# Partition sums of an adaLN modulation: four narrow matmuls and a transposition per 512 columns, or 32x32 block transpositions and one matmul per section

## The chip, the cores and the metric

The kernel runs on one core of a Trainium2 chip. The metric is device time of one execution in microseconds (us). Three runs of the kernel before took 1637.54, 1637.94 and 1638.12 us; their median is 1637.94 us.

## The reference

Two transformer blocks on one sequence of 512 tokens and 1024 features, all in float32. Each block has its own modulation: six vectors of 1024 values (shift, scale and gate for the mixer and for the feed-forward part), from a conditioning vector `c`:

```python
mod = (jax.nn.silu(c) @ w_ada[i] + b_ada[i])[:, None, :]
shift_m, scale_m, gate_m, shift_f, scale_f, gate_f = jnp.split(mod, N_MOD, axis=-1)
h = rmsnorm(x, norm_mix_w[i]) * (1.0 + scale_m) + shift_m
x = x + gate_m * hybrid_mixer(h, ...)
h = rmsnorm(x, norm_mlp_w[i]) * (1.0 + scale_f) + shift_f
x = x + gate_f * (jnp.square(jax.nn.relu(h @ w_up[i])) @ w_down[i])
```

`w_ada` is 1024 x 6144, so a modulation is a vector times a matrix of 25 MB. The second block has the same form, with an mLSTM and sliding-window attention as its mixer and a gated convolutional feed-forward part. The mixer of the first block is a state-space scan (heads of 64 features, chunks of 128 tokens) with a pooling branch.

## The kernel before

Large products are made exact in float32 by splitting each operand into a high and a low part of type float32r: `hilo` (lines 238 to 244) lets ScalarE copy the raw weights into `whi` (L242) and VectorE subtract (L243, `wlo`). `gemm_a` (L273) and `gemm_full` (L351) then issue three matmuls of 512 columns for every 128x128 weight tile. Weights arrive by SyncE's DMA queue in tiles `wraw` of four buffers (`RAW`).

The modulation is a side stream that is fed between the weights. `split_w` calls `pump` after every tile of weights, and every `pump_rate[0]`-th call lets `ada_next` emit one step: a DMA of 512 KB of `w_ada` (four k-tiles of 256 columns, L150) and four VectorE instructions that multiply the rows by the values of `silu(c)` and add them up in an accumulator `adacc` (128 partitions x 256 columns; L154 for the first, L156 for the rest). Two steps make one accumulator of two 128-column pieces. What is left is a sum over the 128 partitions. `ada_sum` does it for four pieces at a time:

```python
for j in range(4):
    PE.matmul(ps[j * 32:(j + 1) * 32, 0:P], lhsT=ones[:, 0:32], rhs=accs[j // 2][:, j % 2 * P:(j % 2 + 1) * P],
              start=True, stop=True)
row = small("colraw", [P, P])
act(out=row, in_=ps[:, 0:P], func=AF.Copy)
```

These are four matmuls with a weight of ones, 32 columns wide, each into its own quarter of the PSUM partitions (L163). Then come a copy on ScalarE (L166), a transposition on TensorE (L169) and an addition of the bias on VectorE (L170) that leaves four columns of `mod`. A section (1024 values) is two such sums. `ada_close` delays sums so that the steps of one lie apart. `ada_until` closes all that is open before a section is used: section 2 of the first block before `GM`, sections 4 and 3 before `g_f`, section 5 before `GF`; sections 0 and 1 of the second block before `gc1`, sections 2, 4 and 3 before `gc2`, section 5 at the end before `G2`. The flag `hold` keeps `gemm_full` from starting new sums, and `ADB - 1` accumulators are the most that may be open, `ADB` being 5.

The shift and scale of the very first normalization are not part of this stream: `first_mod` (L499 to L512) makes them at the start, one pair of pieces for each of eight k-tiles, with two accumulators from the same five buffers and four matmuls (L505).

The tile framework places the instructions of each engine in an order that it plans; every engine runs its own list in order. The front of each norm is of interest below: `front1` (L1024, L1025) adds the gated output of the mixer to `x`, and `h_tile` (L423 to L432) transposes the normalized tokens, scales them and splits them into `hh` (ScalarE) and `hl` (VectorE, L432), which `first_tiles` multiplies by the first weights of the MLP in halves of 256 tokens. Other lines named below: L243 `wlo`, L261 and L357 weight DMAs, L449 the convolution `xs`, L414 the normalized tokens `nx`, L867 the sum of squares over partitions (four full-width float32 matmuls of one column), L1313 a maximum over 512 scores, L1499 the last addition of `post`.

Of the kernel before, what the change touches and what calls it, by code (L numbers as in the profile page):

```python
# [26 lines left out]
def hybrid_kernel(  # L27
# [46 lines left out]
    # ---------------------------------------------------------------- constants  # L74
# [27 lines left out]
    def first_ada(j):  # L102
        """the pieces j of the shift and the scale of the first normalization, four k-tiles at a time."""
        res = []
        for k, tag in ((0, "hi"), (4, "lo")):
            u = wp.tile([P, 4, 2 * P], F32, tag=tag, name="araw")
            for i in range(2):
                dma(out=u[:, :, i * P:(i + 1) * P],
                    in_=w_ada[0, k * P:(k + 4) * P, (8 * i + j) * P:(8 * i + j + 1) * P].rearrange("(k p) n -> p k n", p=P))
            res.append(u)  # L110
        return res
# [29 lines left out]
    # ---------------------------------------------------------------- adaLN modulation  # L141
    mod = [const("mod1", [P, 48]), const("mod2", [P, 48])]
    ada_w, bcol = [w_ada, w_ada_2], [ba_col, None]

    def ada_steps(ci, col):
        """steps that sum the products of the 128-column pieces col and col + 1 of w_ada over their k-tiles."""
        acc = small("adacc", [P, 2 * P], bufs=ADB)
        for k0 in (0, 4):
            raw = RAW([P, 4, 2 * P])
            dma(out=raw, in_=ada_w[ci][0, k0 * P:(k0 + 4) * P, col * P:(col + 2) * P].rearrange("(k p) n -> p k n", p=P))  # L150
            for k in range(4):
                s_ = csil[:, 8 * ci + k0 + k:8 * ci + k0 + k + 1]
                if k0 + k == 0:
                    V.tensor_scalar(out=acc, in0=raw[:, k], scalar1=s_, scalar2=None, op0=ALU.mult)  # L154
                else:
                    V.scalar_tensor_tensor(out=acc, in0=raw[:, k], scalar=s_, in1=acc, op0=ALU.mult, op1=ALU.add)  # L156
            yield acc

    def ada_sum(ci, col, accs):
        """the sums over partitions of four pieces, as columns."""  # L160
        ps = PS("adaps")
        for j in range(4):
            PE.matmul(ps[j * 32:(j + 1) * 32, 0:P], lhsT=ones[:, 0:32], rhs=accs[j // 2][:, j % 2 * P:(j % 2 + 1) * P],  # L163
                      start=True, stop=True)
        row = small("colraw", [P, P])
        act(out=row, in_=ps[:, 0:P], func=AF.Copy)  # L166
        yield
        ps = PS("adaps")
        PE.transpose(ps[:, 0:P], row, ident)  # L169
        V.tensor_tensor(out=mod[ci][:, col:col + 4], in0=ps[:, 0:P:32], in1=bcol[ci][:, col:col + 4], op=ALU.add)  # L170
        yield

    ada_todo = [(0, 8 * sec + i) for sec in (2, 4, 3, 5) for i in range(0, 8, 2)] + [(1, i) for i in range(0, 48, 2)]
    ada_now, ada_open, ada_half = [], [], []
    pump_rate = [0, 0]

    def pump():
        """half a piece of the modulation for every pump_rate[0] tiles of weights."""
        pump_rate[1] += 1
        if pump_rate[0] and pump_rate[1] % pump_rate[0] == 0:  # L180
            ada_next()

    def ada_close(n):
        while ada_half:
            next(ada_half.pop(0))
        while len(ada_open) > max(n, 1):
            (ci, col), a0 = ada_open.pop(0)
            ada_half.append(ada_sum(ci, col, (a0, ada_open.pop(0)[1])))
            next(ada_half[-1])
        while ada_half and n == 0:  # L190
            next(ada_half.pop(0))

    def ada_next(hold=False):
        if ada_now:
            key, gen = ada_now.pop()
            ada_open.append((key, next(gen)))
            return
        if not hold:
            ada_close(3)
        if ada_todo and len(ada_open) < ADB - 1:  # L200
            ci, col = ada_todo.pop(0)
            ada_now.append(((ci, col), ada_steps(ci, col)))
            next(ada_now[0][1])

    def ada_until(ci, sec):
        todo = [(ci, 8 * sec + i) for i in range(0, 8, 2)]
        while any(t in todo for t in ada_todo + [t for t, _ in ada_now]):
            ada_next()
        ada_close(0)

    def cols_to_dram(name, col):
        """[P, n] columns -> n rows in DRAM."""
# [9 lines left out]
    def rows_bcast(name, dr, r0):  # L222
        """four rows of 128 from r0 on, the same in every partition."""
# [4 lines left out]
    def cols_to_rows(name, col):  # L228
        """[P, 8] columns -> two [P, 512] tiles with the vector in every row, by way of DRAM."""
# [8 lines left out]
    # ---------------------------------------------------------------- products  # L238
# [7 lines left out]
    def split_w(parts, kt=8):  # L246
        """weights [kt * 128, 256] (in column parts) -> per k-tile (hi, lo)."""
# [29 lines left out]
    def load_b(wmat, cols, k0):  # L277
        """two k-tiles of the columns [(first, number)] of wmat."""
# [8 lines left out]
    def keep(raw):  # L287
        """weights split into tiles that stay."""
# [10 lines left out]
    def gemm_b(wmat, acts, cols, evac, pairs=((0, 1, 2, 3),), ready=()):  # L299
        """[tokens, columns] products, at most 512 columns, in steps of two k-tiles; with several token groups  # L300
        the weights are held; the first k-tiles of the weights may be there already."""
# [35 lines left out]
    def gemm_full(wmat, acts, evac, tail=4, groups=((0, 1), (2, 3)), before=None, script=None):  # L337
        """[tokens, 1024] products of acts [(row tile, (hi, lo))]; the last `tail` k-tiles go by token
        groups, so that evac(group, pss) of one overlaps the products of the next; before(i) is called
        after k-tile i."""  # L340
# [77 lines left out]
    def h_tile(xh, j, p, ts, gc, bc, on_act=False, bank=PS):  # L418
        """features j of the tokens ts: transposed, scaled, shifted and split into p."""
# [14 lines left out]
    def first_tiles(ws, acts, between=None):  # L434
        """products of the first two 256-column weights, by token halves."""
# [8 lines left out]
    def conv(ps, name, cols, taps, b):  # L444
        """depthwise causal convolution of a [features, tokens] product; cols[k] are [P, 1]."""
# [7 lines left out]
    def silu2(u):  # L453
        """silu(2u), in place."""
# [4 lines left out]
    def log1p_exp_negabs(y, n, name):  # L459
        """log(1 + exp(-|y|)) of [P, n] with the relative accuracy of float32."""  # L460
# [15 lines left out]
    # ================================================================ block 1: mixer  # L476
# [68 lines left out]
    # parameters of the convolution  # L545
# [30 lines left out]
    # time steps: the k-tiles in four column groups of the tensor engine, summed with the transposition  # L576
# [14 lines left out]

    def xbc_items(g):
        """closures that add the convolved tiles of group g to XBC[g]."""
# [19 lines left out]
    # pool branch  # L613
# [30 lines left out]
    # remaining parameters  # L644
# [67 lines left out]
    # time steps  # L712
# [47 lines left out]
    # state-space branch, a group of eight heads at a time  # L760
# [3 lines left out]
    def ssd_decay(g, cc, st):  # L764
        """what chunk cc of group g needs besides the state: scaled inputs, decayed scores, decayed C."""
# [54 lines left out]
    def ssd_out(g, cc, st):  # L820
        """the outputs of chunk cc of group g and the state after it."""
# [32 lines left out]
    def rms_stages(tiles, eps, wcol, name, res):  # L854
        """tiles [features, tokens] -> normed over all their features, scaled by wcol, split, added to res."""
# [43 lines left out]
    def branch_items(g):  # L899
        """the groups g - 1 and g."""  # L900
# [35 lines left out]
    def weave(stages, items):  # L936
        """emits the stages with the items [(cost, step)] spread evenly between them."""
# [760 lines left out]
```

## Time and profile before

| what | value |
|---|---|
| median of three runs | 1637.94 us (1637.54 to 1638.12) |
| profiled execution, first to last instruction (span) | 1635.9 us |
| TensorE (PE), busy | 1605.5 us, 98% |
| TensorE weight loads (PEld), busy | 1293.6 us, 79% |
| VectorE (DVE), busy | 1069.6 us, 65% |
| ScalarE (ACT), busy | 721.2 us, 44% |
| GpSimd (POOL), busy | 28.1 us, 2% |
| chain that ended last | PE 93%, DVE 2%, DMA 2%, ACT 1%, issue 1% |
| mean granted TensorE clock | 0.998 |
| HBM read, written | 202.96 MB, 2.19 MB |

The profile gives the span of the profiled execution and not its own time around it; the median of the runs is 2.04 us above the span. "Busy" of TensorE is modelled from pipelined matmuls, so that consecutive ones overlap in the rows: the step from one start to the next tells what a matmul costs, the duration of one row does not. A float32 matmul is recorded as two rows, a float32r matmul and a transposition as one.

### The profile page before, as it was taken

The numbers are of one execution on the slowest core, as the hardware profiler recorded it, in microseconds if no ns is written. First come the engines' busy times: TensorE is split into PE (matmuls) and PEld (weight loads), VectorE is DVE, ScalarE is ACT, GpSimd is POOL, SyncE is SP. The second block draws the span as 40 slices with busy tenths as digits, with TensorE's granted clock in tenths as the row PEclk, the third lists the DMA queues.
The fourth block names the chain that finished last, engine by engine and source line by source line (L and its number), as shares of the span: only waits on it lengthen the run. The fifth ranks groups of instructions, "written<-read, shape, count | busy, mean of one in ns | idle before, by whom it ended". The sixth has DMA issues, their size and how long they took to land.

```text
span 1635.9 us, 21014 instructions
## 1 busy us (share of the span) xinstructions
PE 1605.5 (98%) x7942; PEld 1293.6 (79%) x7942; DVE 1069.6 (65%) x1944; ACT 721.2 (44%) x1279; POOL 28.1 (2%) x46
## 2 busy tenths in 40 slices
PE   5999999999999999999999999999999999999998
PEld 3778777777877878877877788878888888888886
DVE  6686898889676676875267654584576756245644
ACT  3543665555454333533123333646555544144421
POOL 0000000000000000000000000000001000000000
PEclk9999999999999999999999999999999999999999
DMA  9632544454544444565246571132232333332321
GB/s 284 185 104 66 174 142 142 130 160 132 158 129 142 129 140 144 167 201 185 91 143 194 181 242 27 53 93 62 72 105 71 90 91 103 91 103 82 99 90 52
DMA packets 206762, 206.52 MB, mean 126 GB/s; under 512 B 11397, under 2 KB 184645, under 8 KB 206661
## 3 DMA queue, kind: packets, MB, share of 16 engines
q1 hardware_dynamic: 206661, 205.19, 40.6%
q8 instruction: 62, 1.02, 0.3%
q14 instruction: 39, 0.32, 0.1%
HBM read 202.96 MB, written 2.19 MB: 125 GB/s over the span
## 4 chain that ended last, share of the span: by engine, by line
PE 93%; DVE 2%; DMA 2%; ACT 1%; issue 1%; POOL 0%; SPq 0%; DVEq 0%; POOLq 0%; ACTq 0%
PE ga L273 54%; PE gb L351 21%; PE gb L311 5%; PE go L1480 2%; PE ga L543 2%; DMA wraw<-in_w_ada_dram 1%; PE yps L831 1%; PE ops L1343 1%; PE stps L840 1%; PE nps L423 1%; PE sps L1310 1%; PE yps L836 1%; PE adaps L163 0%; PE xtps L792 0%; PE ptps L1334 0%
## 5 line engine op out<-in xcount | busy, mean ns | idle before, releaser
L243 DVE TENSOR_TENSOR wlo<-wraw,whi 128x1024 fp32r<-128x1024 f32 (+3 forms) x249 | 298.0, 1198 | 256.3 <-ACT whi L242 256.0
L273 PE MATMUL ga<-hh,whi 128*128 128x512 f32 (+1 forms) x1200 | 465.2, 390 | 0.3 <-ACT hh L430 0.3
L273 PE MATMUL ga<-hl,whi 128*128 128x512 f32 (+1 forms) x1200 | 459.2, 384 | 3.0 <-DVE hl L432 2.9
L273 PE MATMUL ga<-hh,wlo 128*128 128x512 f32 (+1 forms) x1200 | 458.0, 382 | 0.0
L242 ACT ACTIVATE whi<-wraw 128x1024 fp32r<-128x1024 f32 (+3 forms) x249 | 257.8, 1036 | 341.2 <-PE ga L273 152.1
L273 PEld LDWEIGHTS ga<-hl,whi 128*128 128x128 f32 x1200 | 226.0, 189 | 52.4 <-DVE hl L432 3.9
L273 PEld LDWEIGHTS ga<-hh,whi 128*128 128x128 f32 x1200 | 224.6, 188 | 53.2 <-issue 6.4
L273 PEld LDWEIGHTS ga<-hh,wlo 128*128 128x128 f32 x1200 | 226.1, 189 | 47.1 <-issue 0.3
L156 DVE SCALAR_TENSOR_TENSOR adacc<-wraw,csil,adacc 128x256 f32<-128x256 f32 x280 | 133.6, 482 | 30.9 <-DMA wraw<-in_w_ada_dram 26.4
L351 PE MATMUL gb<-whi,hidh 128*128 128x512 f32 x240 | 78.2, 396 | 0.0
L351 PE MATMUL gb<-wlo,hidh 128*128 128x512 f32 x240 | 77.8, 395 | 0.0
L351 PE MATMUL gb<-whi,hidl 128*128 128x512 f32 x240 | 77.5, 394 | 0.0
L449 DVE SCALAR_TENSOR_TENSOR xs<-xraw,colB,xs 128x511 f32<-128x511 f32 (+2 forms) x72 | 53.9, 748 | 9.1 <-ACT xs L447 8.3
L351 PE MATMUL gb<-whi,fh 128*128 128x512 f32 x176 | 57.1, 395 | 0.0
L351 PE MATMUL gb<-wlo,fh 128*128 128x512 f32 x176 | 57.1, 394 | 0.0
L351 PE MATMUL gb<-whi,fl 128*128 128x512 f32 x176 | 56.9, 393 | 0.0
L351 PEld LDWEIGHTS gb<-whi,hidh 128*128 128x128 f32 x240 | 45.0, 188 | 10.8 <-issue 0.4
L351 PEld LDWEIGHTS gb<-whi,hidl 128*128 128x128 f32 x240 | 45.1, 188 | 10.7
L351 PEld LDWEIGHTS gb<-wlo,hidh 128*128 128x128 f32 x240 | 45.1, 188 | 10.5
L805 ACT ACTIVATE arel<-AB,acs 128x128 f32<-128x128 f32 x128 | 40.7, 389 | 26.8 <-DMA AB<-acs 18.8
L273 PE MATMUL ga<-yh,whi 128*128 128x512 f32 x128 | 51.3, 401 | 0.0
L273 PE MATMUL ga<-yl,whi 128*128 128x512 f32 x128 | 50.5, 394 | 0.0
(417 smaller groups left out, 2398.3 us busy)
## 6 DMA issues: line engine op xcount, KB each, us to landing
wraw<-in_w_ada_dram SPq DMA_DIRECT2D x80, 512.0 KB
wraw<-in_w_in_dram SPq DMA_DIRECT2D x72, 512.0 KB
wraw<-in_w_down_dram SPq DMA_DIRECT2D x54, 512.0 KB
wraw<-in_w_up_dram SPq DMA_DIRECT2D x88, 256.0 KB
wraw<-in_w_up_dram SPq DMA_DIRECT2D x32, 512.0 KB
araw<-in_w_ada_dram SPq DMA_DIRECT2D x32, 256.0 KB
AB<-acs SPq DMA_DIRECT2D x32, 256.0 KB
wraw<-in_w_branch_ssd_dram SPq DMA_DIRECT2D x16, 512.0 KB
```

Source lines behind the costliest of these rows:

```text
L156: V.scalar_tensor_tensor(out=acc, in0=raw[:, k], scalar=s_, in1=acc, op0=ALU.mult, op1=ALU.add)
L242: act(out=hi, in_=raw, func=AF.Copy)
L243: V.tensor_tensor(out=lo, in0=raw, in1=f(hi), op=ALU.subtract)
L273: PE.matmul(ps[:, n0:n1], lhsT=a[:, m * P:(m + 1) * P], rhs=b[:, n0:n1], start=i == 0, stop=i == 3 * n - 1)
L311: PE.matmul(pss[t][:, 0:ncols], lhsT=a[:, t * P:(t + 1) * P], rhs=b, start=k == 0 and j == 0, stop=k == n - 1 and j == 2)
L351: PE.matmul(pss[t][q], lhsT=a, rhs=w[b][q], start=i == 0 and j == 0, stop=i == n - 1 and j == 2)
L423: PE.transpose(ps[:, i * P:(i + 1) * P], xh[t][j // 4][:, (j % 4) * P:(j % 4 + 1) * P], ident)
L449: V.scalar_tensor_tensor(out=o[:, d:], in0=ps[:, 0:S - d], scalar=cols[taps - 1 - d], in1=o[:, d:], op0=ALU.mult, op1=ALU.add)
L543: PE.matmul(fps[i], lhsT=a[:, i * P:(i + 1) * P], rhs=b, start=j == 0 and q == 0, stop=j == 7 and q == 2)
L805: act(out=t[:, i * P:(i + 1) * P], in_=AB[q][:, i * P:(i + 1) * P], func=AF.Relu, scale=-1.0, bias=acs[:, hh:hh + 1])
L831: PE.matmul(ps[r * 64:(r + 1) * 64, j * P:(j + 1) * P], lhsT=xdt[:, hh * 64:(hh + 1) * 64], rhs=M[hh // 4][:, (hh % 4) * P:(hh % 4 + 1) * ...
L1480: PE.matmul(opss[t][q], lhsT=x_, rhs=w[q][b_], start=half == 0 and k == 0 and j == 0, stop=half == 1 and k == 3 and j == 2)
```

## The change

The partition sum moves from TensorE to VectorE. A unit of the stream is now four pieces in one accumulator of 128 x 512 from the general pool `U` (64 buffers). After its fourth step a VectorE block transposition turns each 32x32 block of the accumulator (`adtr`), and a VectorE reduction adds 32 values each, which leaves 16 columns of `adR`: the sums of each group of 32 partitions. Only when a section is wanted does `ada_until` issue one matmul of 32 columns with a full 128x128 weight `quarters` (made of identity blocks), which adds the four groups for all 1024 values of the section, and three short VectorE instructions: a product with the mask `quarter`, a reduction, the bias. `ada_close`, `ada_sum` and the limit on open accumulators go away, and `hold` no longer has an effect. `first_mod` keeps its form, but `ADB`, the number of its accumulator buffers, falls from 5 to 3. Two small constants are made at the start.

```diff
     def ada_steps(ci, col):
-        acc = small("adacc", [P, 2 * P], bufs=ADB)
-        for k0 in (0, 4):
...
-            yield acc
-
-    def ada_sum(ci, col, accs):
-        ps = PS("adaps")
-        for j in range(4):
-            PE.matmul(ps[j * 32:(j + 1) * 32, 0:P], lhsT=ones[:, 0:32], rhs=accs[j // 2][:, j % 2 * P:(j % 2 + 1) * P],
-                      start=True, stop=True)
-        row = small("colraw", [P, P])
-        act(out=row, in_=ps[:, 0:P], func=AF.Copy)
-        yield
-        ps = PS("adaps")
-        PE.transpose(ps[:, 0:P], row, ident)
-        V.tensor_tensor(out=mod[ci][:, col:col + 4], in0=ps[:, 0:P:32], in1=bcol[ci][:, col:col + 4], op=ALU.add)
-        yield
+        acc = U("adacc")
+        for h in range(2):
+            a = acc[:, h * 2 * P:(h + 1) * 2 * P]
+            for k0 in (0, 4):
...
+                if h and k0:
+                    tr = U("adtr")
+                    V.transpose(out=tr, in_=acc)
+                    V.tensor_reduce(out=adR[ci][:, col * 4:col * 4 + 16], in_=tr.rearrange("p (b f) -> p b f", f=32),
+                                    axis=AX.X, op=ALU.add)
+                yield
...
     def ada_next(hold=False):
+        if not ada_now and ada_todo:
+            ci, col = ada_todo.pop(0)
+            ada_now.append([4, (ci, col), ada_steps(ci, col)])
         if ada_now:
-            key, gen = ada_now.pop()
-            ada_open.append((key, next(gen)))
-            return
-        if not hold:
-            ada_close(3)
-        if ada_todo and len(ada_open) < ADB - 1:
-            ci, col = ada_todo.pop(0)
-            ada_now.append(((ci, col), ada_steps(ci, col)))
-            next(ada_now[0][1])
+            next(ada_now[0][2])
+            ada_now[0][0] -= 1
+            if ada_now[0][0] == 0:
+                ada_now.pop()
...
     def ada_until(ci, sec):
-        todo = [(ci, 8 * sec + i) for i in range(0, 8, 2)]
-        while any(t in todo for t in ada_todo + [t for t, _ in ada_now]):
+        todo = [(ci, 8 * sec), (ci, 8 * sec + 4)]
+        while any(t in todo for t in ada_todo + [n[1] for n in ada_now]):
             ada_next()
-        ada_close(0)
+        ps = PS("adaps")
+        PE.matmul(ps[:, 0:32], lhsT=quarters, rhs=adR[ci][:, sec * 32:sec * 32 + 32], start=True, stop=True)
+        own = small("adown", [P, 32])
+        V.tensor_tensor(out=own.rearrange("p (c j) -> p c j", j=4), in0=ps[:, 0:32].rearrange("p (c j) -> p c j", j=4),
+                        in1=quarter.unsqueeze(1).to_broadcast([P, 8, 4]), op=ALU.mult)
+        m = mod[ci][:, 8 * sec:8 * sec + 8]
+        V.tensor_reduce(out=m, in_=own.rearrange("p (c j) -> p c j", j=4), axis=AX.X, op=ALU.add)
+        V.tensor_tensor(out=m, in0=m, in1=bcol[ci][:, 8 * sec:8 * sec + 8], op=ALU.add)
...
+    quarters, quarter = const("quarters", [P, P]), const("quarter", [P, 4])
+    V.tensor_copy(out=quarters.rearrange("p (j f) -> p j f", f=32), in_=sel.unsqueeze(1).to_broadcast([P, 4, 32]))
+    V.tensor_reduce(out=quarter, in_=ident.rearrange("p (j f) -> p j f", f=32), axis=AX.X, op=ALU.add)
...
+ADB = 3
-ADB = 5
```

The planned order of the instructions changes with it. Three places matter below. In the changed file, L195 is the new matmul, L164 and L165 the block transposition and the reduction, L159 and L161 the accumulation, L424 `hl`, L1021 and L1022 `front1`; the other numbers are lower by three to eight than before.

First, TensorE where the first half of the MLP's up-projection of block 1 ends and its down-projection begins (near 753 us of the profiled span). Before:

```order
L273 MATMUL ga<-hl,whi 128x512
L273 MATMUL ga<-hh,wlo 128x512
L169 MATMUL adaps<-consts,colraw 128x128
L163 MATMUL adaps<-adacc,ones 32x128 x4
L351 MATMUL gb<-whi,hidh 128x512
```

And in the changed kernel:

```order
L265 MATMUL ga<-hl,whi 128x512
L265 MATMUL ga<-hh,wlo 128x512
L195 MATMUL adaps<-adR_117,quarters 128x32
L343 MATMUL gb<-whi,hidh 128x512
L343 MATMUL gb<-wlo,hidh 128x512
```

The transposition and the four narrow matmuls are gone; one matmul for the whole section stands in their place. In the long rows of `ga` products before this place, where sums stood every 24 to 48 products, nothing stands any more.

Second, VectorE where the MLP of block 1 starts (near 657 us). Before, one accumulation step stands between the scaled tokens `ntmp` and their low part `hl`:

```order
L414 TENSOR_SCALAR nx<-x,nr 128x512
L243 TENSOR_TENSOR wlo<-wraw,whi 128x1024 x2
L431 TENSOR_SCALAR ntmp<-nps,gc_f,mod_115 128x256
L156 SCALAR_TENSOR_TENSOR adacc<-wraw,csil,adacc 128x256
L432 TENSOR_TENSOR hl<-ntmp,hh 128x256
L1024 TENSOR_TENSOR tmp<-gb,gm 128x512 x2
```

In the changed kernel:

```order
L406 TENSOR_SCALAR nx<-x,nr 128x512
L235 TENSOR_TENSOR wlo<-wraw,whi 128x1024
L423 TENSOR_SCALAR ntmp<-nps,gc_f,mod_115 128x256
L424 TENSOR_TENSOR hl<-ntmp,hh 128x256
L1021 TENSOR_TENSOR tmp<-gb,gm 128x512 x2
L1022 TENSOR_TENSOR x<-x,tmp 128x512 x2
L235 TENSOR_TENSOR wlo<-wraw,whi 128x1024
```

The accumulation step has moved behind this piece, `hl` follows `ntmp` at once, and one of the two `wlo` has moved behind the four additions of `front1`.

Third, VectorE in the state-space branch (near 242 us), where the first block transposition lies in the changed kernel:

```order
L782 TENSOR_TENSOR scm<-scps,consts 128x512
L791 TENSOR_TENSOR xdt<-xtps,dt 128x512
L795 TENSOR_TENSOR xdd<-xtps,dS 128x512
L164 STREAM_TRANSPOSE adtr<-adacc 128x512
L698 SCALAR_TENSOR_TENSOR gp<-gp,ga 128x512
L165 TENSOR_REDUCE adR_117<-adtr 128x16
L806 TENSOR_TENSOR arel<-arel,scm 128x512
```

Before, `arel` (the decayed scores that the products `yps` wait for) had one accumulation step and a `wlo` in front of it here; now it has the pair of the transposition and the reduction.

## Rows read from the trace of the kernel before

**Rows 1.** The page's span and its busy time by engine.
```profile
span 1635.9 us, 21014 instructions
PE 1605.5 (98%) x7942; PEld 1293.6 (79%) x7942; DVE 1069.6 (65%) x1944; ACT 721.2 (44%) x1279; POOL 28.1 (2%) x46
```

**Rows 2.** Who TensorE waited for: us in total, times, longest (two of its rows).
```profile
PE adaps L505 <- DVE adacc L501: 5.9, 1, 5.9
...
PE ga L273 <- DVE hl L432: 2.9, 2, 2.6
```

**Rows 3.** The lines of the sum: ns shortest/median/longest, first and last start in us, shapes.
```profile
L163 PE MATMUL adaps<-adacc,ones x160: 272/273/297, 298.4 to 1201.9; 128*32 128x128 f32 x160
L169 PE MATMUL adaps<-consts,colraw x20: 270/271/307, 328.8 to 1205.0; 128*128 128x128 f32 x20
```

**Rows 4.** TensorE's timeline around one sum: start us, us, line, operation, shape, records.
```profile
350.80 0.39 PE L273 MATMUL ga<-hh,wlo 128*128 128x512 f32 x1
351.11 0.43 PE L163 MATMUL adaps<-adacc,ones 128*32 128x128 f32 x8
351.47 0.50 PE L273 MATMUL ga<-hh,whi 128*128 128x512 f32 x1
351.81 0.40 PE L273 MATMUL ga<-hl,whi 128*128 128x512 f32 x1
352.04 0.39 PE L273 MATMUL ga<-hh,wlo 128*128 128x512 f32 x1
```

**Rows 5.** The same around two sums in a row.
```profile
605.97 0.39 PE L273 MATMUL ga<-yh,wlo 128*128 128x512 f32 x1
606.29 0.64 PE L163 MATMUL adaps<-adacc,ones 128*32 128x128 f32 x16
606.87 0.50 PE L351 MATMUL gb<-whi,mxh 128*128 128x512 f32 x1
607.20 0.39 PE L351 MATMUL gb<-wlo,mxh 128*128 128x512 f32 x1
```

**Rows 6.** The same around one transposition.
```profile
706.69 0.40 PE L273 MATMUL ga<-hh,wlo 128*128 128x512 f32 x1
706.94 0.27 PE L169 MATMUL adaps<-consts,colraw 128*128 128x128 f32 x1
706.96 0.49 PE L273 MATMUL ga<-hh,whi 128*128 128x512 f32 x1
707.29 0.40 PE L273 MATMUL ga<-hl,whi 128*128 128x512 f32 x1
```

**Rows 7.** The same around four full-width float32 matmuls of one column.
```profile
284.71 0.40 PE L273 MATMUL ga<-hh,wlo 128*128 128x512 f32 x1
284.94 0.95 PE L867 MATMUL ssps<-ones,ysq 128*128 128x1 f32 x8
...
286.07 0.39 PE L273 MATMUL ga<-hl,whi 128*128 128x512 f32 x1
```

**Rows 8.** VectorE's groups by shape: busy us, mean ns of one, idle before and releaser.
```profile
L1499 DVE SCALAR_TENSOR_TENSOR xw<-py,nr,xw 128x512 f32<-128x512 f32 x16 | 11.3, 748 | 4.3 <-POOL nr L395 4.1
...
L1313 DVE TENSOR_REDUCE amx<-sps 128x2 f32<-128x512 f32 x12 | 8.1, 688 | 2.0 <-PE sps L1310 2.0
...
L414 DVE TENSOR_SCALAR nx<-x,nr 128x512 f32<-128x512 f32 x12 | 5.5, 484 | 4.1 <-POOL nr L395 4.1
```

**Rows 9.** VectorE's timeline where the MLP of block 1 starts.
```profile
660.17 0.48 DVE L156 SCALAR_TENSOR_TENSOR adacc<-wraw,csil,adacc 128x256 f32<-128x256 f32 x1 [2.24 <-DMA wraw<-in_w_ada_dram]
660.57 0.42 DVE L432 TENSOR_TENSOR hl<-ntmp,hh 128x256 fp32r<-128x256 f32 x1
```

**Rows 10.** Stretches: PE, PEld, DVE, ACT, POOL busy (count), granted clock, DMA share, GB/s.
```profile
160.00:260.00 100.00, 99.92 (x542) 79.27 (x541) 87.10 (x145) 63.05 (x123) 0.00 (x0) 1.00 0.50 153
658.00:661.00 3.00, 0.42 (x3) 0.18 (x2) 0.83 (x3) 0.00 (x0) 0.00 (x0) 0.93 0.92 293
661.00:664.00 3.00, 2.96 (x14) 2.96 (x15) 3.00 (x7) 1.18 (x4) 0.00 (x0) 0.51 0.35 121
```

More of the change, by code (lines that the diff above doesn't have):

```diff
@@ L143, in hybrid_kernel @@
     ada_w, bcol = [w_ada, w_ada_2], [ba_col, None]
+    adR = [const("adR1", [P, 192]), const("adR2", [P, 192])]
     def ada_steps(ci, col):
-        acc = small("adacc", [P, 2 * P], bufs=ADB)
-        for k0 in (0, 4):
[L149 to L156, printed above, removed]
-            yield acc
@@ L173, in hybrid_kernel @@
-    ada_todo = [(0, 8 * sec + i) for sec in (2, 4, 3, 5) for i in range(0, 8, 2)] + [(1, i) for i in range(0, 48, 2)]
-    ada_now, ada_open, ada_half = [], [], []
+        acc = U("adacc")
+        for h in range(2):
+            a = acc[:, h * 2 * P:(h + 1) * 2 * P]
+            for k0 in (0, 4):
+                raw = RAW([P, 4, 2 * P])
+                dma(out=raw, in_=ada_w[ci][0, k0 * P:(k0 + 4) * P, (col + 2 * h) * P:(col + 2 * h + 2) * P].rearrange("(k p) n -> p k n", p=P))
+                for k in range(4):
+                    s_ = csil[:, 8 * ci + k0 + k:8 * ci + k0 + k + 1]
+                    if k0 + k == 0:
+                        V.tensor_scalar(out=a, in0=raw[:, k], scalar1=s_, scalar2=None, op0=ALU.mult)
+                    else:
+                        V.scalar_tensor_tensor(out=a, in0=raw[:, k], scalar=s_, in1=a, op0=ALU.mult, op1=ALU.add)
+                if h and k0:
[4 more added lines that the diff above has]
+                yield
@@ L175, in hybrid_kernel @@
+    ada_todo = [(0, 8 * sec + i) for sec in (2, 4, 3, 5) for i in (0, 4)] + [(1, i) for i in range(0, 48, 4)]
+    ada_now = []
     pump_rate = [0, 0]
@@ L181, in pump @@
             ada_next()
[L183 to L191, printed above, removed]
     def ada_next(hold=False):
+        if not ada_now and ada_todo:
+            ci, col = ada_todo.pop(0)
+            ada_now.append([4, (ci, col), ada_steps(ci, col)])
         if ada_now:
-            key, gen = ada_now.pop()
-            ada_open.append((key, next(gen)))
-            return
-        if not hold:
-            ada_close(3)
-        if ada_todo and len(ada_open) < ADB - 1:
-            ci, col = ada_todo.pop(0)
-            ada_now.append(((ci, col), ada_steps(ci, col)))
-            next(ada_now[0][1])
+            next(ada_now[0][2])
+            ada_now[0][0] -= 1
+            if ada_now[0][0] == 0:
+                ada_now.pop()
     def ada_until(ci, sec):
-        todo = [(ci, 8 * sec + i) for i in range(0, 8, 2)]
-        while any(t in todo for t in ada_todo + [t for t, _ in ada_now]):
+        todo = [(ci, 8 * sec), (ci, 8 * sec + 4)]
+        while any(t in todo for t in ada_todo + [n[1] for n in ada_now]):
             ada_next()
-        ada_close(0)
+        ps = PS("adaps")
[6 more added lines that the diff above has]
+        V.tensor_tensor(out=m, in0=m, in1=bcol[ci][:, 8 * sec:8 * sec + 8], op=ALU.add)
     def cols_to_dram(name, col):
```

## The prediction

> **What bounds the kernel.** I read the page's busy times first: TensorE is busy for 1605.5 us of a span of 1635.9, VectorE for 1069.6 [rows 1]. The kernel is bound by TensorE almost everywhere, so what counts is what TensorE no longer has to issue, and whether VectorE, which takes the work over, is ever late. The second view is the list of TensorE's waits [rows 2]: for VectorE's accumulator at the start it waits once, 5.9 us, and for `hl` twice, 2.9 us, of which one wait is 2.6. The third is the groups of the two lines that go [rows 3], the fourth TensorE's timeline. There the durations overlap, so I take the distance from one start to the next: an ordinary `ga` product of 512 columns steps by 352.04 - 351.81 = 0.23 us [rows 4], and what an inserted group costs is the distance across it less that many steps. Last come VectorE's shapes, its timeline around the 2.6 us, and busy shares by stretch [rows 8 to 10].
>
> The sum is made against the profiled execution's span of 1635.9 us. The median of the runs, 1637.9, is 2.0 above it, and I carry that distance over unchanged: all savings are taken from 1637.9.
>
> **TensorE: what goes.** The 160 records of L163 are 80 matmuls, 20 sums of four; the 20 transpositions of L169 go too [rows 3]. In the timeline 14 of the sums stand alone and six in three pairs. One alone: 351.81 - 350.80 = 1.01 us with two products in it, so 1.01 - 2 x 0.23 = 0.55 [rows 4]. A pair: 607.20 - 605.97 = 1.23, less 0.46, 0.77 [rows 5]. A transposition: 707.29 - 706.69 = 0.60, less 0.46 and some hundredths for rounding, 0.12 [rows 6]; against 0.27 in its own row. So 14 x 0.55 + 3 x 0.77 + 20 x 0.12 = 7.7 + 2.3 + 2.4 = 12.4 us go, all on the path, since TensorE is busy where they lie. The record's own 272 ns would have made 160 x 0.27 = 43 us, which is why I don't use it.
>
> **TensorE: what comes.** Ten matmuls with a full 128x128 weight and 32 columns, in six places (1, 2, 1, 2, 3 and 1 of them). The nearest rows are four full-width float32 matmuls of one column: 286.07 - 284.71 = 1.36, less 0.46, 0.90 for four [rows 7]. I take 0.2 each and 0.1 more for each place, 10 x 0.2 + 6 x 0.1 = 2.6 us. Below, they could hardly be cheaper than the transposition, 10 x 0.12 = 1.2 [rows 6]; above, two records of 0.27 each laid end to end [rows 3], 10 x 0.54 + 0.6 = 6.0. I stay near the first because it is the same kind of instruction with a weight of the same size. Net: -12.4 + 2.6 = **-9.8 us** (between -11.2 and -6.4).
>
> **The wait at 658 us.** One accumulation step stands in front of `hl` on VectorE and waits 2.24 us for its `w_ada` transfer; `hl` follows at 660.57 [rows 9], and TensorE, which needs it, idles for the 2.6 us of [rows 2] (busy 0.42 of 3.00 us [rows 10]). In the three microseconds after it the granted clock is 0.51 [rows 10], that is the lower of the two levels, 1.2 GHz, after an idle stretch; 2.96 busy us at it hold what about half the time would hold at 2.4 GHz, so another 1.4 us go with the idle time. In the changed order the step stands behind `hl` and the additions of `front1`, and `hl` follows `ntmp` at once. I count the whole wait as gone, **-4.0 us**. Late next would be the `wlo` that moved behind `front1`: four instructions of 0.6 us later (1.28 for two), some 2.5 us. Its products come in the second half of the same weights, so I cost that at nothing; the cover is the time that the first half's products take. If it is too thin, the wait comes back at up to 2.5 us. The gain is between 0 and 4.0.
>
> **VectorE: what comes.** Twenty block transpositions of 128x512 and twenty reductions of 512 to 16 values, 30 short instructions and two constants against 20 short additions that go. No row shows a block transposition. Its bounds are the row of one source, `nx` with 484 ns, and the one of two sources, `xw` with 748 [rows 8]; I take the lower, since it reads one tile and writes one. The reduction has a row of the same input size, 688 ns [rows 8]. A pair is 1.17 us (at most 1.44), twenty are 23.4 us on an engine with 1635.9 - 1069.6 = 566 us free. A pair costs nothing where VectorE runs ahead of TensorE. It is least ahead in the state-space branch: 87.10 of 100 us busy from 160 to 260 [rows 10], and one pair now stands ahead of `arel`, for which the products `yps` wait. Three pairs fall into the 200 us from 160 on. Nothing there shows slack of over a microsecond, nor that none is left, so I take half of three: 3 x 1.17 / 2 = **+1.8 us** (0 to 3.5, and 23.4 if every pair delayed TensorE).
>
> The short instructions behind a section's matmul stand on the way of the next `gm` or `gc`, as the copy, the transposition and the addition did, one hop less; nothing. The constants are made while VectorE waits for the first transfers; nothing. ScalarE loses 20 copies and is not waited for at these places; nothing.
>
> **Buffers and queues.** The first phase has three accumulators in place of five; the two of one k-tile still fit, and a third piece may begin before the oldest is summed. TensorE's one wait there is 5.9 us, for the first one [rows 2], which no later buffer can delay. Cost nothing, with the 5.9 as the most if the wait came back a second time. With `hold` without effect, SyncE's queue gets `w_ada` loads a little earlier in the output and down projections, ahead of some weights. In the fullest stretch above the DMA share is 0.50 [rows 10], so a load of half a megabyte should find room. Nothing, unless it takes a buffer that a weight needs, which would look like the wait at 658 us at another place.
>
> **Sum.** 1637.9 - 9.8 - 4.0 + 1.8 = **1626** us.
>
> **Rivals.** *The wait at 658 stays or turns up elsewhere*: the earlier `w_ada` loads make other steps wait in front of something urgent, or the late `wlo` takes over. Then 1637.9 - 9.8 + 1.8 = 1630 us. For it: that wait came from an order that a planner made without knowing when the transfer lands, and the order is made anew for all 20 units. Against: it was one such wait among 80 steps of accumulation that share their queue with the weights.
>
> *VectorE becomes the bound for a stage*: the slower side. If each pair delayed the instruction behind it, and that one TensorE, 20 x 1.17 = 23.4 us would come against 13.8 gone: 1637.9 - 13.8 + 23.4 = 1648 us; with the dearer pair of 1.44, 1653. It decides from 13.8 / 20 = 0.7 us of delay per pair on. For it: 87% in the fullest stretch. Against: outside the start TensorE waited for VectorE's `hl` for 2.9 us alone [rows 2], and with two thirds of its time used VectorE usually is ahead.
>
> *The narrow matmuls run side by side*: each of the four writes its own quarter of the partitions with a quarter of the columns. If such matmuls took the time of one full-width matmul, a sum would be 0.90 / 4 = 0.22 us of work [rows 7], and the other 0.33 of its 0.55 a gap that could stay with whatever stands there. Then 20 x 0.22 + 2.4 - 2.6 = 4.2 us are saved on TensorE and the time is 1637.9 - 4.2 - 4.0 + 1.8 = 1632 us. Against: nothing stands in 28 of the 34 places any more, and the next two starts are the usual step apart.
> The Trainium skill, page "TensorEngine Tiling (Array Packing)", section "Overview", has it so: a matmul with a small dimension of at most 32 is given a speed-up of up to four times, because the array works as independent tiles. By that rule the sums were already the cheap form and the new full-width matmul is the dear one; the trace agrees only in part, as a pair costs 0.77 where eight matmuls one after another would cost 1.8.
>
> *Nothing measurable*: TensorE's time is modelled; the products behind a sum might run closer together, so that what goes is given back as waits for weights. 1637 us. Against: at a step of 0.23 us the products before and after a sum run at the same pace [rows 4].
>
> **How the numbers follow.** About 0.2% (3.3 us) is what a measurement of this kernel can tell from no change. Forecast 1626: 0.60. Wait stays: 0.20. Side by side: 0.06. Nothing: 0.08. Slower: 0.06. The first three lie below 1634.6, so faster has 0.86, same 0.08, slower 0.06. The range: at the low end net -11.2, -4.0 and no delay by the pairs give 1622.7; the 1.7 us down to 1621 are left for the order of the accumulations elsewhere, which no row prices. At the high end -6.4, no gain at 658 and three full pairs give 1637.9 - 6.4 + 3.5 = 1635; all three at once is less likely than 1 in 10, two of them end at 1633. I set 1621 to 1633.
>
> **What would show it.** Right: no rows of L163 and L169; at the six places the new matmuls insert 0.2 to 0.3 us; TensorE's wait for `hl` is below 0.5 us and the clock is 1.00 where it was 0.51; VectorE's busy time is up by some 20 to 25 us and its share from 160 to 260 is near 90; TensorE's other waits are the same. Wrong: a transposition of over a microsecond, a TensorE wait for `yps`, `wlo` or `hl` that was not there, a `w_ada` wait in front of one of these, or TensorE's busy time down by clearly less than the distance of the times.

## The result, and the profile after

| what | before | after |
|---|---|---|
| median | 1637.74 us (1636.68 to 1638.12, 4 runs) | 1627.47 us (1626.03 to 1628.46, 4 runs) |
| span of the profiled execution | 1635.9 us | 1624.3 us |

The ratio is 0.9937, with a 95% interval of 0.9925 to 0.9949: 8 to 12 us faster. The predicted time was 1626.0, its range 1621 to 1633. In a second series (e5, five runs of the changed kernel) it took 1625.54 us against 1637.35, a ratio of 0.9931 (0.9919 to 0.9944). So two series of one kernel differ by 2 us, and no difference below that is read from medians alone; where a time went is read from the traces, by the start of the same matmul in both.

The page's busy time in the changed kernel, to be held against [rows 1]:

```profile
PE 1595.5 (98%) x7782; PEld 1290.3 (79%) x7782; DVE 1089.6 (67%) x1996; ACT 717.7 (44%) x1259; POOL 27.4 (2%) x46
```

TensorE has 10.0 us less to do and VectorE 20.0 us more. What TensorE waited for: two rows that answer to [rows 2], and one that is new (us, times, longest):

```profile
PE adaps L497 <- DVE adacc L493: 6.0, 1, 6.0
...
PE ga L265 <- DVE hl L424: 0.6, 2, 0.3
...
PE ga L265 <- DVE wlo L235: 0.3, 1, 0.3
```

The wait at the start is the same, so the fourth and fifth small buffer were not missed. The 2.6 us wait for `hl` is gone. New are this wait for `wlo`, at 215 us, and one of 0.3 us of `yps` for `arel`, at 190; the prediction named such waits as signs of being wrong, but both are short and lie before the first pair. The new lines, by shape (ns shortest/median/longest, first and last start):

```profile
L195 PE MATMUL adaps<-adR,quarters x20: 191/276/276, 512.9 to 1555.0; 128*128 128x32 f32 x20
L164 DVE STREAM_TRANSPOSE adtr<-adacc x20: 702/705/714, 247.6 to 927.4; 128x512 f32<-128x512 f32 x20
L165 DVE TENSOR_REDUCE adR<-adtr x20: 671/678/686, 248.8 to 929.2; 128x16 f32<-128x512 f32 x20
```

The reduction has the duration of the row that it was priced by (688 ns [rows 8]); the transposition, at 705 ns, is near the two-source row of 748, not at the 484 that I took. TensorE's timeline at the one place with a single section matmul:

```profile
743.89 0.40 PE L265 MATMUL ga<-hh,wlo 128*128 128x512 f32 x1
744.12 0.30 PE L195 MATMUL adaps<-adR,quarters 128*128 128x32 f32 x2
744.26 0.48 PE L343 MATMUL gb<-whi,hidh 128*128 128x512 f32 x1
744.58 0.39 PE L343 MATMUL gb<-wlo,hidh 128*128 128x512 f32 x1
```

It inserts 744.58 - 743.89 - 0.46 = 0.23 us; the six places together 2.2 us.

VectorE where the MLP of block 1 starts, to be held against [rows 9]: `hl` follows `ntmp` at once, with nothing in front of it.

```profile
653.64 0.54 DVE L423 TENSOR_SCALAR ntmp<-nps,gc_f,mod 128x256 f32<-128x256 f32 x1
654.21 0.43 DVE L424 TENSOR_TENSOR hl<-ntmp,hh 128x256 fp32r<-128x256 f32 x1
654.56 1.28 DVE L1021 TENSOR_TENSOR tmp<-gb,gm 128x512 f32<-128x512 f32 x2
```

The stretches that answer to [rows 10] (PE, PEld, DVE, ACT, POOL busy with counts, granted clock, DMA share, GB/s):

```profile
160.00:260.00 100.00, 99.47 (x533) 78.26 (x533) 82.56 (x136) 61.46 (x121) 0.00 (x0) 1.00 0.47 139
...
655.00:665.00 10.00, 9.81 (x77) 8.90 (x75) 7.87 (x17) 6.30 (x15) 0.55 (x1) 1.00 0.38 127
```

In the second, the granted clock is 1.00 (2.4 GHz) where it was 0.51. VectorE's share from 160 to 260 us fell from 87.10 to 82.56, where I had expected about 90: only the first pair lies there, and the stream starts later, so that eight accumulation instructions and two `wlo` fewer do.

Matched by TensorE's matmuls, the changed kernel is this far ahead (-) or behind of the kernel before; the first column is the time in the kernel before:

| at (us) | shift (us) | what lies in between |
|---|---|---|
| 120 | +0.4 | the first phase |
| 240 | +2.0 | nothing removed yet; among others a `wlo` late by 0.4 us |
| 605 | -2.1 | six sums gone, one section's matmul new |
| 680 | -6.8 | two sums and the wait at 658 gone, two matmuls new |
| 840 | -9.2 | four sums gone, one matmul new |
| 935 | -11.9 | four sums gone |
| 1320 | -13.0 | the last four sums gone, five matmuls new |
| end | -11.6 | the last new matmul, and a slow drift back |

Of the 2.0 us at 240 not all is the change's. Up to 620 us the kernels e1, e6, e9 and e11 below have the kernel before's order on every engine, and their traces are 0.9 to 1.7 us behind its own at 245; those of the changed kernel and of its variants e3, e4, e8, e10 and e12 are 1.6 to 2.8. So about 1 us is left for the change.

The late `wlo` at 214 us stands behind accumulation steps on VectorE that did not stand there before:

```profile
213.07 0.48 DVE L161 SCALAR_TENSOR_TENSOR adacc<-wraw,csil,adacc 128x256 f32<-128x256 f32 x1
213.47 0.75 DVE L441 SCALAR_TENSOR_TENSOR xs<-xraw,colB,xs 128x510 f32<-128x510 f32 x1
214.13 1.22 DVE L235 TENSOR_TENSOR wlo<-wraw,whi 128x1024 fp32r<-128x1024 f32 x1
```

### The profile page after: what moved, and what is told of

It reads as the page before. It is cut to its first block, busy times and chain, and to the rows that moved or that the text cites. A ratio compares the mean times of both kernels' runs of the same rounds, so it can differ in the third digit from the quotient of the medians.

```text
span 1624.3 us, 20710 instructions
## 1 busy us (share of the span) xinstructions
PE 1595.5 (98%) x7782; PEld 1290.3 (79%) x7782; DVE 1089.6 (67%) x1996; ACT 717.7 (44%) x1259; POOL 27.4 (2%) x46
## 3 DMA queue, kind: packets, MB, share of 16 engines
HBM read 202.96 MB, written 2.19 MB: 126 GB/s over the span
## 4 chain that ended last, share of the span: by engine, by line
PE 92%; DVE 3%; DMA 2%; ACT 1%; issue 1%; SPq 0%; POOL 0%; DVEq 0%; POOLq 0%; ACTq 0%
PE ga L265 55%; PE gb L343 21%; PE gb L303 5%; PE ga L535 2%; PE go L1477 2%; PE yps L828 1%; PE ops L1340 1%; PE stps L837 1%; PE nps L415 1%; PE yps L833 1%; DMA wraw<-in_w_ada_dram 1%; PE sps L1307 0%; DVE wlo L235 0%; DMA x<-in_x_dram 0%; PE xtps L789 0%
## 5 line engine op out<-in xcount | busy, mean ns | idle before, releaser
L161 DVE SCALAR_TENSOR_TENSOR adacc<-wraw,csil,adacc 128x256 f32<-128x256 f32 x280 | 130.5, 481 | 15.6 <-DMA wraw<-in_w_ada_dram 13.0
```

The lines of the kernel that those rows point to most:

```text
L161: V.scalar_tensor_tensor(out=a, in0=raw[:, k], scalar=s_, in1=a, op0=ALU.mult, op1=ALU.add)
```

## The experiments

The kernel before took 1637.3 to 1637.8 us beside them.

**What TensorE's sums cost: e2.** The kernel before without its sums on TensorE.

```diff
-        ps = PS("adaps")
-        for j in range(4):
-            PE.matmul(ps[j * 32:(j + 1) * 32, 0:P], ...
...
-        act(out=row, in_=ps[:, 0:P], func=AF.Copy)
+        act(out=row, in_=accs[1][:, 0:P], func=AF.Copy)
...
-        PE.transpose(ps[:, 0:P], row, ident)
-        V.tensor_tensor(out=mod[ci][:, col:col + 4], in0=ps[:, 0:P:32], ...
+        V.tensor_tensor(out=mod[ci][:, col:col + 4], in0=row[:, 0:P:32], ...
```

> The kernel before without the 80 narrow matmuls and the 20 transpositions; the copy and the addition of the bias stay, with wrong values (the partition sums are left out). The accumulation step in front of hl stays. Theory (a sum costs 0.55 us, one in a pair 0.39, a transposition 0.12): 12.4 us less, 1625.3 us, with the wait for hl of 2 to 3 us still there. Rival (narrow matmuls run side by side, 0.22 us of work per sum): 6.8 us less, 1631 us. Rival (the time is refilled by waits): 1637 us.

Measured: 1626.06 us against 1637.33, 11.3 less (ratio 0.9931, 0.9919 to 0.9944, that is 9 to 13 us). The order at 658 us is as before, and its wait is still there:

```profile
PE ga L267 <- DVE hl L426: 2.3, 2, 2.0
```

So the price by start-to-start distances, 12.4 us, holds within the interval, and a saving of 6.8 is excluded. What is excluded is the rival's time, not its picture of the matmuls. In the trace of the kernel before, the eight records of the sum in [rows 4] start in two rounds, four within 0.02 us at 351.11 and four within 0.02 at 351.25, while the full-width records of [rows 7] start 0.11 us apart: the narrow matmuls do run side by side. The rest of the 0.55 us lies before, between and behind the two rounds, where TensorE starts nothing; why, is not shown. The rival let this rest stay when the matmuls go, and e2 shows that it went with them. The Trainium skill, page "TensorEngine Tiling (Array Packing)", section "Overview", lists up to four times for a small dimension of at most 32; the trace agrees for the starts, but what the group costs between full-width products is 0.55 us, against 0.90 for four full-width matmuls of one column [rows 4, 7].

**What the pairs cost: e3 and e4.** The changed kernel without its pairs, and with each made twice.

```diff
-                    tr = U("adtr")
-                    V.transpose(out=tr, in_=acc)
-                    V.tensor_reduce(out=adR[ci][:, col * 4:col * 4 + 16], ...
+                    V.tensor_copy(out=adR[ci][:, col * 4:col * 4 + 16], in_=acc[:, 0:16])
```

> The changed kernel with each block transposition and its reduction replaced by one copy of 16 columns (the sums of 32 partitions are left out). Theory (VectorE's new work is hidden but for about half of three pairs): 0 to 3.5 us less than the changed kernel, 1625.7 us at 1.8. Rival (each pair delays TensorE): 23 us less, about 1604 us. Rival (it is hidden altogether and the time given back from 160 to 300 us comes from the new order): no difference, 1627.5.

```diff
+                    for twice in range(2):
                         tr = U("adtr")
                         V.transpose(out=tr, in_=acc)
                         V.tensor_reduce(...)
```

> The changed kernel with each block transposition and its reduction made twice. Theory: VectorE has 28 us more to do, of which 0 to 4 us show, 1629 us. Rival (each pair delays TensorE): 27 us more, about 1655 us.

Measured: e3 1624.64 us, ratio to the kernel before 0.9922 (0.9910 to 0.9935); e4 1629.06, ratio 0.9952 (0.9940 to 0.9964). The changed kernel stands between them with 0.9931 and 0.9937, so that twenty pairs, 27.7 us of VectorE's time, read as 1.5 to 2.5 us and twenty more as 2.5 to 3.4. The slower rival is excluded. But the intervals of e3 and of the changed kernel overlap, and the traces give the pairs less. e3 gains 0.8 us on the changed kernel between 664 and 668 us and gives back 0.3 at 749; 1.1 of the 1.4 us by which it is ahead at the end (0.9 against the second profile of the changed kernel) it gains evenly behind 1220 us, where the changed kernel has no pair, by the pace of the plain products (see the last section). e4 loses 1.2 us at 666 and 1.0 at 749, which is nearly all of its 2.3. So the traces show pairs to cost time where the MLP starts, and when doubled at 749 us too, and neither is where I put it. At the MLP's start the changed kernel has a pair among the `hl`:

```profile
662.40 0.42 DVE L424 TENSOR_TENSOR hl<-ntmp,hh 128x256 fp32r<-128x256 f32 x1 [1.02 <-ACT hh L420]
662.75 0.70 DVE L164 STREAM_TRANSPOSE adtr<-adacc 128x512 f32<-128x512 f32 x1
663.38 0.31 DVE L159 TENSOR_SCALAR adacc<-wraw,csil 128x256 f32<-128x256 f32 x1
663.61 0.68 DVE L165 TENSOR_REDUCE adR<-adtr 128x16 f32<-128x512 f32 x1
...
664.59 0.54 DVE L423 TENSOR_SCALAR ntmp<-nps,gc_f,mod 128x256 f32<-128x256 f32 x1
```

In e3 `ntmp` follows sooner:

```profile
662.52 0.43 DVE L421 TENSOR_TENSOR hl<-ntmp,hh 128x256 fp32r<-128x256 f32 x1 [1.04 <-ACT hh L417]
662.86 0.35 DVE L159 TENSOR_SCALAR adacc<-wraw,csil 128x256 f32<-128x256 f32 x1
663.12 0.54 DVE L420 TENSOR_SCALAR ntmp<-nps,gc_f,mod 128x256 f32<-128x256 f32 x1
```

It starts 0.60 us after that `hl`, in the changed kernel 2.19, and TensorE there waits 0.3 us for the next `hl`. From 240 to 360 us, where the first pairs lie and I had charged 1.8 us, e3 gains nothing: at 245 us it is 2.2 us behind the kernel before, as the changed kernel is, so what is lost by then is not the pairs'.

**The wait at 658 us: e1, e6, e9, e11.** All four are the kernel before with the stream paused at the start of the first MLP, so that `hl` there waits for no transfer.

```diff
             c0 = half * 2048 + q * 256
+            pump_rate[0] = int(half > 0 or q > 3)
```

> The kernel before, with the modulation's stream paused over the first four weight tiles of the first MLP, so that no accumulation step stands in front of hl where that MLP starts (both wlo stay where they were). Theory (the wait was worth the idle time and the low clock behind it): 4.0 us less than the kernel before, 1633.7 us; TensorE's wait for hl below 0.5 us and the granted clock 1.00 from 655 to 665. Rival (TensorE's products behind the wait have slack in their weights' transfers, so that the time is given back): the wait is gone from the trace but the time is within 1 us of 1637.7.

Measured: 1636.3 us against 1637.33, ratio 0.9995 (0.9986 to 1.0004), so neither theory's time. In the traces the shift against the kernel before goes from +1.5 to -2.2 us across the place, 3.7 gained, and back from -3.3 to -0.1 between 1045 and 1220: 32 of the 320 accumulation instructions now lie behind 1000 us, where the kernel before has none. Two of the 20 sums and their transpositions have moved there too, from before 753 us, some 1.3 of the 3.2 us at the prices above; TensorE's new waits of over 0.2 us in this stretch add up to 1.0. The rest I have not located. The next kernels make the steps up.

```diff
+            pump_rate[0] = 0 if half == 0 and q <= 3 else 1
...
+            if half == 0 and q > 3:
+                ada_next()
+                ada_next()
```

> As e1_no_wait, but the eight steps that the pause leaves out are made up for in the second half of the same product's weights, so that the stream ends no later than in the kernel before. Theory (in e1 the wait of 4 us was gained at 658 us and 3 us were given back between 1045 and 1205 us, because accumulation steps had moved into the second block): 4.0 us less than the kernel before, 1633.5 us, and no loss from 1045 to 1205. Rival (the gain is lost again further on whatever the stream does): within 1 us of e1, 1636.3 us.

Measured: 1637.71 us against 1637.35, ratio 1.0005 (0.9996 to 1.0014). Again 3.7 us gained at 658, and 6 lost at 753. That is the profiled execution, which at 1640.28 us was 2.6 above the median; the median, 0.4 above the kernel before, leaves some 4 for the loss. TensorE's waits, and the two stretches behind them:

```profile
PE adaps L169 <- ACT colraw L166: 1.4, 1, 1.4
PE gb L351 <- DVE mod L170: 1.3, 1, 1.3
```

```profile
753.00:756.00 3.00, 1.42 (x4) 0.98 (x5) 2.04 (x6) 0.52 (x3) 0.00 (x0) 0.70 0.78 251
756.00:759.00 3.00, 3.00 (x8) 2.31 (x7) 3.00 (x7) 0.63 (x1) 0.00 (x0) 0.50 0.81 245
```

`ada_until` closes everything that is open, also accumulators that were finished a moment ago; copy, transposition and addition then run one after another with TensorE waiting, and after that the granted clock is 0.50 (1.2 GHz). e9 makes the steps up in the second half instead:

```diff
+            if half == 1 and 2 <= q < 6:
+                ada_next()
+                ada_next()
```

> As e6_no_wait_caught_up, but the eight steps are made up for in the second half of the MLP, well after the sums that are closed at 753 us. Theory (the wait at 658 us is worth 4 us, and in e6 the 6 us lost at 753 us came from closing sums whose steps had just been moved there): 4 us less than the kernel before, 1633.4 us, no loss at 753 and none from 1045 on. Rival (a pause always costs what it gains): within 1 us of 1637.4 us.

Measured: 1640.15 us against 1637.81, ratio 1.0015 (1.0006 to 1.0024), slower. The loss had moved with the steps, to the closing at 935 us:

```profile
937.94 0.69 PE L169 MATMUL adaps<-consts,colraw 128*128 128x128 f32 x2 [3.23 <-ACT colraw L166]
```

e11 pauses over two tiles only and is even again after two more:

```diff
+            pump_rate[0] = 0 if half == 0 and q in (2, 3) else 1
...
+            if half == 0:
+                for _ in range({4: 2, 5: 2}.get(q, 0)):
+                    ada_next()
```

> The kernel before, with the stream paused over the third and fourth weight tile of the first MLP only and its four steps made up for with the fifth and sixth, so that the sums that are closed at 753 and 935 us find their accumulators as early as in the kernel before. Theory (the wait at 658 us is worth 4 us; e1, e6 and e9 lost it where they had moved accumulations in front of a closing of sums): 4 us less than the kernel before, 1633.7 us, a shift of 4 us at 665 us that stays to the end. Rival (a pause always costs what it gains): 1637.7 us.

Measured: 1634.83 us against 1637.61, 2.8 less (ratio 0.9982, 0.9973 to 0.9990, that is 1.6 to 4.4 us). In the traces the shift goes from +1.1 to -2.5 across the place and stays at -2.6 to -2.8 to the end. The 1.1 had been there since 245 us, in a stretch in which the two kernels are the same. All four paused kernels have a new wait just behind the place:

```profile
PE nps L423 <- ACT ntmp L427: 0.7, 1, 0.7
```

Before it the shift is -2.7, so the wait itself was worth 3.9 us and taking it away in this manner 3.6. The rival that a pause always costs what it gains is excluded.

**The changed kernel with the same pauses: e8 and e10.** Their edits are those of e6 and e9.

> The changed kernel with the stream paused over the first four weight tiles of the first MLP and made up for in the next four, so that no transposition, reduction or accumulation step lies among the hl of that MLP's start. Theory (the pair at 663 us there delays hl and costs TensorE about 1 us; the other pairs are hidden): 1 us less than the changed kernel, 1626.5 us, and VectorE's 0.3 us waits for hl gone. Rival (all of the changed kernel's cost of pairs lies elsewhere): same as the changed kernel, 1627.5 us.

> As e8_after_paused, with the eight steps made up for in the second half of the MLP. Theory (in e8 1 us was gained behind 663 us, where the first pair had stood between the hl, and lost again at 745 us, where the steps made up for stood in front of the gate of the MLP): 1 us less than the changed kernel of the series before, 1625 us, without the loss at 745 us. Rival (the pair at 663 us was covered): the same as the changed kernel, 1626 to 1627 us.

Measured: e8 1626.55 us, ratio 0.9940 (0.9928 to 0.9952); e10 1626.39, ratio 0.9926 (0.9912 to 0.9939); the changed kernel in e8's series 1625.54, 0.9931. No gain, against my theory. In the traces both gain 0.6 us on the changed kernel behind 663 us, where I had 1 us, but lose 1.0 just before, since the pause brings the wait for `ntmp` here too. Further on other waits follow, in e8 at 748 us for the short instructions behind a section's matmul, which stand behind other work on VectorE:

```profile
PE rowps L207 <- DVE mod L201: 1.0, 1, 1.0
PE nps L415 <- ACT ntmp L419: 0.8, 1, 0.8
```

and in e10 at 901 to 903 us for the two parts of one weight tile:

```profile
PE ga L265 <- ACT whi L234: 0.7, 1, 0.7
PE ga L265 <- DVE wlo L235: 0.7, 1, 0.7
```

What they do show: where the same moves cost the kernel before 6 us in its profiled executions (e6 at 753, e9 at 938), the changed one loses 1.2 (e8) and 2.0 (e10). In the code a section's matmul needs its own section alone and not all that is open, and in no trace does TensorE wait over 0.2 us for it; that this is the reason is argued, not tested.

**The first phase's buffers: e7 and e12.**

```diff
-        acc = [small("adacc", [P, 2 * P], bufs=ADB) for _ in range(2)]
+        acc = [U("adacc")[:, 0:2 * P] for _ in range(2)]
```

> The changed kernel with the first phase's accumulators taken from the general pool of 64 buffers in place of three small ones. Theory (the small buffers cost nothing): within 1 us of the changed kernel, 1627.5 us. Rival (the third buffer is missed in the first phase): up to 6 us less, 1621.5 us, with a shorter wait for the first accumulators.

Measured: 1641.88 us, 16 more than the changed kernel in the same series and slower than the kernel before (ratio 1.0033, 1.0020 to 1.0045). I had expected at most a gain. With many buffers the planner puts the first accumulation behind all of the normalized tokens. VectorE in e7:

```profile
18.30 0.88 DVE L406 TENSOR_SCALAR nx<-x,nr 128x512 f32<-128x512 f32 x2 [0.66 <-POOL nr L387]
...
19.10 0.61 DVE L491 TENSOR_SCALAR adacc<-araw,csil 128x256 f32<-128x256 f32 x2
```

and in the changed kernel, where it starts as soon as its transfer lands:

```profile
6.76 0.62 DVE L491 TENSOR_SCALAR adacc<-araw,csil 128x256 f32<-128x256 f32 x2 [1.19 <-DMA araw<-in_w_ada_dram]
```

TensorE's wait for it grows from 6.0 to 17.2 us (first row):

```profile
PE adaps L497 <- DVE adacc L493: 17.2, 1, 17.2
PE ga L535 <- ACT hh L420: 11.5, 8, 2.1
```

Its waits for `hh` grow by 9.5 us as well, and the 6.3 for `nx` go; together that is 14.4 of the 15.5 us between the two spans.

So the second part of the change is not only thrift with memory: small buffers keep the order of the first phase.

```diff
-ADB = 3
+ADB = 2
```

> The changed kernel with two small buffers for the first phase's accumulators in place of three. Theory (three are enough since VectorE waits for data there, two make the accumulation of a k-tile wait for the sum of the one before): 1 to 6 us more than the changed kernel, 1627 to 1633 us. Rival (the buffers' number matters only through the planner's order): no difference, 1626.5 us.

Measured: 1627.12 us, ratio 0.9935 (0.9922 to 0.9949). Its trace is 0.7 and 1.1 us behind the two of the changed kernel from 220 us on, no more than runs of one kernel differ there, so it does not decide between theory and rival; two buffers would nearly do. No kernel here is measurably faster than the changed one.

## Why the prediction was right

The time was right to 1.5 us (to 0.5 in the second series). The two large terms were right by their mechanism; the small ones came out by luck in part:

- **TensorE, what goes**, -12.4 us: right. e2 measured 11.3 (9 to 13), with the wait still in place, though 0.6 shorter, and a new one of 1.1 for `yps` at 498 us.
- **TensorE, what comes**, +2.6: right, 2.2 in the trace. The nearest row, the full-width matmuls of one column, priced it well.
- **The wait at 658 us**, -4.0: right. The trace shows a step of -4.2 between 656 and 680 us, with the pair's delay at 663 already in it; e11 has 3.6 to 3.9. The late `wlo` did not take its place. It is a gain of the planned order and not of the sums: e11 has it with every sum in place. That it is not simply there for any edit that moves the step was not in my reasoning: e6 and e9 lost it again at a later closing of sums, e1 where its steps had moved to.
- **VectorE's pairs**, +1.8: within what e3 and e4 allow, but not shown, and for a wrong reason. I charged the state-space stage because VectorE is fullest there, and no pair costs anything there. What the traces locate is 0.8 us at 664 to 668, where VectorE's average is lower but a pair stood in front of `ntmp`. That the sum came out as near as it did is in part luck: the time that the 1.8 stood for was lost by terms that were not in the sum. The price of a transposition was too low by 0.2 us, and it did not matter.
- **Buffers and queues**, nothing: right for three against five; the bounds of 0 to 5.9 us missed that the number sets the planner's order (16 us in e7). That the stream runs in another order shows as one `wlo` late by 0.4 us at 214.
- **Not in the sum**: the changed kernel is 2.0 us behind by 240 us, about half of which executions of the kernel before differ by among themselves, and it drifts back by 1.3 behind 1220 us (1.5 with the last new matmul), of open cause. By the trace, 13.0 us of sums and transpositions gone, 2.2 of matmuls new, 4.2 at 658 with the pair in it, 2.0 and 1.3: -13.0 + 2.2 - 4.2 + 2.0 + 1.3 = -11.7, against -11.6 between the two spans.

The rivals: VectorE as the bound fell with e4, nothing measurable with the result. Of *side by side* the time fell with e2; its picture, that the four narrow matmuls run at once, is what the trace of the kernel before shows. *The wait stays or turns up elsewhere* did not come true here, but it is what happened in e6 and e9.

## What to carry to other kernels

On a full TensorE, price what goes by the distance of starts around it, not by its rows, and look at the new order for the one wait that the old one had placed in front of something urgent: it was worth a third of the gain, and here the planner gave it, not the removal. Work moved to another engine costs where it stands in front of an instruction that is waited for, whatever that engine's average load there. And the number of buffers of a pool can decide a planned order: try a small one before a large one.

## What was not expected of the hardware

The plain products of 512 columns do not run at quite the same pace in all kernels, in a stretch in which TensorE never waits over 0.2 us. From 1320 to 1420 us the mean distance of some 430 starts is 232.75, 232.73 and 232.75 ns in three profiled runs of nearly the same program (the changed kernel twice and e12), 232.20 in the kernel before, and 231.91, 231.93 and 231.93 in e8, e10 and e3; the granted clock reads 1.00 in these. Behind 1220 us that is the drift of 1.3 us above, and most of what e3 is ahead. It repeats with the program, so it is hardly chance; its cause stays open.

A 32x32 block transposition of 128x512 takes VectorE 705 ns, and the next instruction starts 0.63 us after it. The Trainium skill, page "Vector Engine (DVE) Microarchitecture Reference", section "The reshape front-end and per-opcode configuration", says that it sustains one element per cycle and lane. No run here shows the engine's cycle; what the traces show is 512 elements of a lane in 0.63 us, and a duration nearer to the two-source row of the same size (748 ns) than to the one-source row (484) [rows 8].

TensorE's clock fell to the lower level after idle stretches of 2.6 us (kernel before), 2.0 (e2), 3.2 (e9) and of 1.4 and 1.3 close together (e6). It did not in the changed kernel after the 0.3 us in front of `hl`, nor in e4 after one of 1.3 at 667 us, nor in e10 after 0.7 and 0.7 at 902.
